# Two residual blocks on one core: the scatter matmuls of an expert group move into the next group's first product

## The chip, the core and the metric

The kernel runs on one core of a Trainium2 chip. The metric is the time of one execution on the device, in microseconds; the number compared is the median of several runs. The engines are TensorE (PE, with its weight loads as PEld), VectorE (DVE), ScalarE (ACT), GpSimd (POOL) and SyncE (SP, whose queue issues nearly all loads from HBM). The engines run side by side and wait for each other through semaphores; each takes its own instructions in the order in which they were written out for it.

## The reference, cut to what matters

The reference has two blocks of two layers each, on 256 tokens of width 1024. The change touches only the mixture of experts that ends each layer of the second block. Its first layer applies it to two streams, the latent one (`x`) and the context (`xc`); its second and last layer to the latent stream alone.

```python
def expert_choice_ffn(h, w_router, w_g, w_u, w_d):
    cap = CAPACITY_FACTOR * n // N_EXPERTS            # 32 tokens for each of 16 experts
    aff = jax.nn.softmax(jnp.einsum('bnd,de->ben', h, w_router), axis=1)
    gate, idx = lax.top_k(aff, cap)
    xs = h[bi, idx]
    a = jnp.einsum('becd,edf->becf', xs, w_g)
    u = jnp.einsum('becd,edf->becf', xs, w_u)
    y = jnp.einsum('becf,efd->becd', jax.nn.silu(a) * u, w_d)
    return jnp.zeros_like(h).at[bi, idx].add(y * gate[..., None])
...
x = x + gt2 * expert_choice_ffn(h2, ...)
```

All of it is float32. Each expert has three weight matrices of 1024 x 1024, so a layer's experts are 192 MB (16 x 3 x 4 MB) that are read once.

## The kernel before, in words

**Groups, products, steps.** The 16 experts go in four groups of four (`GE`), `gi` from 0 to 3. A group has three products: gate (`w_e_gate`), up (`w_e_up`) and down (`w_e_down`). A product runs over the contraction in four steps (`kp`, L1280); in a step there is one weight tile of 1024 KB for each of the four experts. On each tile stand, for each stream `s`, four matmuls (two rows of blocks `k`, two halves `n` of the output's 1024 columns), so with two streams a step has 32 matmuls and with one 16.

**Quarters.** An expert has 32 tokens, so a matmul (L1290) has 32 columns of weights: it fills a quarter of the array, and expert `e` of the group always has quarter `e`, its result in rows 32e to 32e+31 of an accumulator. A stream has two accumulators of 512 columns; with two streams three come from the pool `acc` (three buffers) and one from `mm`.

**Between the products.** ScalarE takes the silu of the gate product (L1303, recorded at L278 in the helper `act`), VectorE multiplies it by the up product (L1312), TensorE transposes the result (L1316) and ScalarE copies it (L1317); that is the left side of the down product.

**The scatter.** ScalarE copies the down product into `ys` (L1332), a buffer of the pool `k4`, for each stream. `scatter` (L1321) then adds it into the stream: for each of eight blocks `k` of 128 features one matmul of `ys` with the map of this group (L1324; the map holds each token's gate at its slot, 128 x 256), full array width, into one of three buffers `dd`, and one VectorE instruction that multiplies by the modulation and adds to `x` or `xc` (L1325). With two streams there are 16 of them behind a group's down product, with one 8. The last group (L1336) goes another way: its down product is made in four column pieces, with the scatter of two blocks per stream behind each.

**The loads.** `expert_loads` makes the list of 192 tiles in the order in which they are used, and the ring of buffers that they go to (`w`, `k8`, `hh`, `hl`, and pairs of half tiles in `k4`). `self.more` (L1284) issues them on SP (L1249). SP's queue is in order: a load that waits for its buffer holds all that are behind it.

**What sets the order.** The code is not run in the order written: a scheduler of the framework orders the instructions of each engine by its own estimate of when each may start, with the code's order as the tie. So where a matmul stands on TensorE is read from the built order and not from the code.

The names below: `w`, `k`, `hh`, `hl` on the right of an arrow of L1290 are weight tiles, `wl` the transposed left side of the down product, `k` or `pt` behind the comma the gathered tokens of the context and of the latent stream.

Of the kernel before, what the change touches and what calls it, by code (L numbers as in the profile page):

```python
# [13 lines left out]
OP = mybir.AluOpType  # L14
# [3 lines left out]
P = 128  # L18
S = 256
D = 1024  # L20
KT = D // P
# [113 lines left out]
class Kernel:  # L135
# [1138 lines left out]
    def experts(self, l, groups, gather, done):  # L1274
        nc, io = self.nc, self.io
        ns = len(groups)

        def product(which, gi, lhs):
            accs = [[self.acc(), self.acc()], [self.acc(), self.mm()]] if ns == 2 else [[self.acc(), self.acc()]]
            for kp in range(4):  # L1280
                if gather and which == 0 and gi == 0:
                    for _ in range(3 if kp == 0 else 2):
                        next(gather)
                self.more(max(0, GE - len(self.loaded)))  # L1284
                tiles = [self.loaded.pop(0) for _ in range(GE)]
                for s in range(ns):
                    for k in range(2):
                        for n in range(2):
                            for e in range(GE):
                                nc.tensor.matmul(accs[s][n][32 * e:32 * e + 32], lhs(s, 2 * kp + k, e),  # L1290
                                                 tiles[e][k][:, 512 * n:512 * n + 512],
                                                 start=kp == 0 and k == 0, stop=kp == 3 and k == 1,
                                                 skip_group_check=True)
            return accs

        for gi in range(N_EXP // GE):
            pick = lambda s, k, e: groups[s][2][k // 4][:, k % 4, (GE * gi + e) * CAP:(GE * gi + e + 1) * CAP]
            acts, actt = [], []
            pa = product(0, gi, pick)
            for s in range(ns):  # L1300
                a = self.wh([P, D], F32)
                for n in range(2):
                    self.act(a[:, 512 * n:512 * n + 512], pa[s][n], AF.Silu)  # L1303
                acts.append(a)
            pu = product(1, gi, pick)
            if gi == 0:
                maps = [self.gate_map(g[3]) for g in groups]
            for s in range(ns):
                tt = self.wl([P, KT, P], F32)
                for n in range(2):  # L1310
                    a = acts[s][:, 512 * n:512 * n + 512]
                    nc.vector.tensor_tensor(a, a, pu[s][n], op=OP.mult)  # L1312
                    ps = self.dd((P, 4, P))
                    for i in range(4):
                        b = slice(i * P, (i + 1) * P) if gi == N_EXP // GE - 1 else self.paired(i)
                        nc.tensor.transpose(ps[:, i], a[:, b], self.c("ident"))  # L1316
                    nc.scalar.copy(tt[:, 4 * n:4 * n + 4], ps)  # L1317
                actt.append(tt)
            down = lambda s, k, e: actt[s][:, k, 32 * e:32 * e + 32]

            def scatter(s, k, y):  # L1321
                x, gate, _, _ = groups[s]
                ps = self.dd()
                nc.tensor.matmul(ps, y[:, k * P:(k + 1) * P], maps[s][:, gi], start=True, stop=True)  # L1324
                nc.vector.scalar_tensor_tensor(x[:, k], ps, gate[:, k:k + 1], x[:, k], op0=OP.mult, op1=OP.add)  # L1325

            ys = [self.k4([P, D]) for _ in range(ns)]
            if gi < N_EXP // GE - 1:
                py = product(2, gi, down)
                for s in range(ns):  # L1330
                    for n in range(2):
                        nc.scalar.copy(ys[s][:, 512 * n:512 * n + 512], py[s][n])  # L1332
                    for k in range(KT):
                        scatter(s, k, ys[s])
                continue
            for q in range(4):  # L1336
                self.more(max(0, GE - len(self.loaded)))
                tiles = [self.loaded.pop(0) for _ in range(GE)]
                for s in range(ns):
                    ps = self.acc((P, S))  # L1340
                    for k in range(KT):
                        for e in range(GE):
                            nc.tensor.matmul(ps[32 * e:32 * e + 32], down(s, k, e), tiles[e][k], start=k == 0,
                                             stop=k == KT - 1, skip_group_check=True)
                    nc.scalar.copy(ys[s][:, 256 * q:256 * q + 256], ps)
                    for k in range(2 * q, 2 * q + 2):
                        scatter(s, k, ys[s])
                    for k in range(2 * q, 2 * q + 2):
                        done(s, k)

# [179 lines left out]
```

## Time and profile before

| | us |
|---|---|
| median of 3 runs | 2745.01 (2744.41 to 2746.25) |
| the profiled execution | 2746.57 |
| its span, first to last instruction | 2744.8 |
| TensorE matmul busy | 2556.2 (93%) |
| TensorE weight loads busy | 1813.3 (66%) |
| VectorE busy | 1361.8 (50%) |
| ScalarE busy | 1079.1 (39%) |

The experts of layer 0 run from about 1455 to 1960 us of the span, those of layer 1 from about 2320 to the end. A busy share is an average: matmuls overlap in the pipeline and, where they fill only a quarter of the array, run beside each other, so "busy" says that at least one quarter has work. An idle time is put down to what ended it; "issue" is idle time that ends without anything that the profile shows.

### The profile page before, as it was taken

How to read it: one execution, taken by the hardware profiler on the slowest of the kernel's cores; microseconds unless marked ns; L12 is line 12 of the kernel's file. 1: busy time of each engine (PE TensorE's matmuls, PEld its weight loads, DVE VectorE, ACT ScalarE, POOL GpSimd, SP SyncE). 2: the span in 40 equal slices, each digit the busy share in tenths (PEclk: the TensorE clock that was granted, in tenths of full speed). 3: DMA queues.
4: the chain of work that ended last, by engine and by line, in shares of the span. 5: the costliest groups of instructions: out<-in, count | busy, mean ns of one | idle time of the engine just before them, and what ended most of it. 6: DMA issues, size and time to landing. Idle time of an engine off the chain costs nothing.

```text
span 2744.8 us, 45167 instructions
## 1 busy us (share of the span) xinstructions
PE 2556.2 (93%) x18730; PEld 1813.3 (66%) x18730; DVE 1361.8 (50%) x2607; ACT 1079.1 (39%) x2073; POOL 74.9 (3%) x84
## 2 busy tenths in 40 slices
PE   7998999999999999989999999999989998888877
PEld 5998998888998789868983333333578993222222
DVE  5989977757777855787551011010487552000001
ACT  4665555555556744566452000000476442000000
POOL 0000000001000000100021000000000001000000
PEclk8999999999999999999999999999999999999998
DMA  8887954677555578423656999999732776999999
GB/s 320 273 308 272 332 174 155 206 285 256 174 186 181 194 247 282 146 78 116 184 187 239 357 409 398 425 380 410 270 108 96 220 247 261 425 424 425 424 425 323
DMA packets 315004, 742.66 MB, mean 271 GB/s; under 512 B 16215, under 2 KB 212783, under 8 KB 275119
## 3 DMA queue, kind: packets, MB, share of 16 engines
q1 hardware_dynamic: 313710, 738.72, 72.8%
q8 instruction: 148, 2.42, 0.3%
q10 hardware_dynamic: 1088, 1.05, 0.1%
q14 instruction: 58, 0.47, 0.0%
HBM read 738.67 MB, written 1.05 MB: 269 GB/s over the span
## 4 chain that ended last, share of the span: by engine, by line
PE 72%; DMA 16%; DVE 5%; ACT 4%; issue 1%; SPq 1%; POOL 0%; ACTq 0%; DVEq 0%; POOLq 0%
PE dd L254 36%; PE acc L1290 11%; PE mm L1290 5%; PE acc L254 3%; DMA k<-in_w_e_down_dram 3%; DMA w<-in_w_e_up_dram 3%; DMA k<-in_w_e_up_dram 2%; DMA k<-in_w_e_gate_dram 2%; DMA w<-in_w_e_down_dram 2%; DMA w<-in_w_e_gate_dram 2%; PE mm L1001 2%; PE ad L415 2%; ACT k L278 1%; ACT wh L236 1%; PE mm L995 1%; PE acc L973 1%
## 5 line engine op out<-in xcount | busy, mean ns | idle before, releaser
L237 DVE TENSOR_TENSOR wl<-w,wh 128x1024 fp32r<-128x1024 f32 (+1 forms) x534 | 553.1, 1038 | 282.4 <-ACT wh L236 272.9
L254 PE MATMUL dd<-hh,wh 128*128 128x256 f32 x2384 | 679.2, 287 | 14.8 <-ACT hh L278 11.7
L236 ACT CAST wh<-w 128x1024 fp32r<-128x1024 f32 (+1 forms) x534 | 479.0, 901 | 516.6 <-PE dd L254 379.4
L254 PE MATMUL dd<-hl,wh 128*128 128x256 f32 x2384 | 674.2, 283 | 1.7 <-DVE hl L500 1.7
L254 PE MATMUL dd<-hh,wl 128*128 128x256 f32 x2384 | 674.3, 283 | 0.6 <-DVE wl L237 0.6
L254 PEld LDWEIGHTS dd<-hh,wh 128*128 128x128 f32 x2384 | 451.3, 190 | 35.8 <-ACT hh L278 13.2
L254 PEld LDWEIGHTS dd<-hl,wh 128*128 128x128 f32 x2384 | 452.9, 190 | 6.5 <-DVE hl L500 2.7
L254 PEld LDWEIGHTS dd<-hh,wl 128*128 128x128 f32 x2384 | 452.5, 190 | 4.7 <-issue 2.8
L1290 PE MATMUL acc<-w,pt 128*32 128x512 f32 x624 | 223.4, 601 | 30.3 <-DMA w<-in_w_e_up_dram 16.4
L1312 DVE TENSOR_TENSOR wh<-wh,acc 128x512 f32<-128x512 f32 x20 | 13.7, 687 | 451.4 <-PE acc L1290 451.4
L1290 PE MATMUL acc<-k,pt 128*32 128x512 f32 x692 | 224.9, 598 | 8.6 <-DMA k<-in_w_e_up_dram 5.2
L254 PE MATMUL dd<-k,wh 128*128 128x256 f32 x896 | 163.5, 283 | 0.0
L1290 PE MATMUL acc<-w,k 128*32 128x512 f32 x480 | 159.9, 600 | 0.7 <-ACT pt L1187 0.7
L1290 PE MATMUL acc<-w,wl 128*32 128x512 f32 x396 | 139.7, 599 | 13.9 <-DMA w<-in_w_e_down_dram 13.9
L1290 PE MATMUL acc<-k,wl 128*32 128x512 f32 x432 | 146.4, 599 | 4.6 <-DMA k<-in_w_e_down_dram 4.6
L254 PEld LDWEIGHTS dd<-k,wh 128*128 128x128 f32 x896 | 137.5, 188 | 3.3 <-ACT pt L278 1.3
L1290 PE MATMUL acc<-k,k 128*32 128x512 f32 x376 | 134.1, 606 | 0.0
L1290 PEld LDWEIGHTS acc<-w,pt 128*32 128x32 f32 x624 | 46.0, 110 | 133.0 <-issue 69.9
L254 PE MATMUL dd<-k,wl 128*128 128x256 f32 x448 | 125.5, 280 | 0.0
L1325 DVE SCALAR_TENSOR_TENSOR x_res<-dd,mod,x_res 128x256 f32<-128x256 f32 x64 | 28.9, 483 | 171.4 <-PE dd L1324 171.3
L1290 PEld LDWEIGHTS acc<-k,pt 128*32 128x32 f32 x692 | 45.9, 109 | 95.4 <-issue 64.3
L1317 ACT COPY wl<-dd 128x512 f32<-128x512 f32 x24 | 13.2, 591 | 242.7 <-PE dd L1316 242.7
(361 smaller groups left out, 4441.1 us busy)
## 6 DMA issues: line engine op xcount, KB each, us to landing
w<-in_w_in_dram SPq DMA_DIRECT2D x104, 1024.0 KB
w<-in_w_ada_dram SPq DMA_DIRECT2D x63, 1024.0 KB
w<-in_w_e_gate_dram SPq DMA_DIRECT2D x54, 1024.0 KB
w<-in_w_e_up_dram SPq DMA_DIRECT2D x54, 1024.0 KB
w<-in_w_e_down_dram SPq DMA_DIRECT2D x48, 1024.0 KB
w<-in_w_up_dram SPq DMA_DIRECT2D x44, 1024.0 KB
k<-in_w_e_gate_dram SPq DMA_DIRECT2D x43, 1024.0 KB
k<-in_w_e_down_dram SPq DMA_DIRECT2D x43, 1024.0 KB
```

Of the source, the lines that this page charges most:

```text
L236: self.nc.scalar.copy(h, src)
L237: self.nc.vector.tensor_tensor(l, src, h.bitcast(F32), op=OP.subtract)
L254: self.last_mm = self.nc.tensor.matmul(ps, a, b, start=first and i == 0, stop=last and i == len(ops) - 1, skip_group_check=group)
L278: i = self.nc.scalar.activation(out, in_, func, **kw)
L415: nc.tensor.matmul(ad[32 * g:32 * g + 32], cs[:, 2 * c + j], t[:, j, 256 * g:256 * g + 256], start=j == 0 and (c == 0 or not hold), stop=j ...
L973: nc.tensor.matmul(ps[:, :n], q[:, f, mt, qb * P:(qb + 1) * P], kk[br][i][:, f, lo:512], start=i == 0, stop=i == 1 and not mask, skip_grou ...
L995: nc.tensor.transpose(pp[:, i], e[:, i * P:(i + 1) * P], self.c("ident"))
L1001: nc.tensor.matmul(po[64 * f:64 * f + 64], vv[:, kt, P * br + 64 * f:P * br + 64 * f + 64], pt[:, f, i], start=i == 0, stop=i == len(kts) ...
L1290: nc.tensor.matmul(accs[s][n][32 * e:32 * e + 32], lhs(s, 2 * kp + k, e), tiles[e][k][:, 512 * n:512 * n + 512], start=kp == 0 and k == 0, ...
L1312: nc.vector.tensor_tensor(a, a, pu[s][n], op=OP.mult)
L1317: nc.scalar.copy(tt[:, 4 * n:4 * n + 4], ps)
L1325: nc.vector.scalar_tensor_tensor(x[:, k], ps, gate[:, k:k + 1], x[:, k], op0=OP.mult, op1=OP.add)
```

## The change

The scatter of a group that is not the last is no longer written behind its down product. The 16 (or 8) of them are put in a list, block by block and with the streams in turn, and `product` takes a quarter of the list after each of its steps: four per step with two streams, two with one. The next product is the next group's gate product, so all are written within its four steps. `scatter` moves out of the loop and takes the group's number; the last group's scatters are called as before.

```diff
                                                  skip_group_check=True)
+                for _ in range(min(len(rest), KT * ns // 4)):
+                    scatter(*rest.pop(0))
             return accs
+
+        rest = []
+
+        def scatter(gi, s, k, y):
+            x, gate, _, _ = groups[s]
+            ps = self.dd()
+            nc.tensor.matmul(ps, y[:, k * P:(k + 1) * P], maps[s][:, gi], start=True, stop=True)
+            nc.vector.scalar_tensor_tensor(x[:, k], ps, gate[:, k:k + 1], x[:, k], op0=OP.mult, op1=OP.add)
...
                     for n in range(2):
                         nc.scalar.copy(ys[s][:, 512 * n:512 * n + 512], py[s][n])
-                    for k in range(KT):
-                        scatter(s, k, ys[s])
+                rest += [(gi, s, k, ys[s]) for k in range(KT) for s in range(ns)]
                 continue
...
-                        scatter(s, k, ys[s])
+                        scatter(gi, s, k, ys[s])
```

What the scheduler makes of it on TensorE, in layer 0, between the down product of group 0 and the gate product of group 1. Before, the last three of the 16 scatters and what follows them; the four tiles of the step are `w_17872`, `w_17874`, `k_3122_17876` and `k_3123_17878`:

```order
L1324 MATMUL dd_17859<-k_3062_17597,k_3078_17649 128x256
L1324 MATMUL dd_17862<-k_3062_17597,k_3078_17649 128x256
L1324 MATMUL dd_17865<-k_3062_17597,k_3078_17649 128x256
L1290 MATMUL acc_17868<-w_17872,k_2926_16882 32x512
L1290 MATMUL acc_17868<-w_17874,k_2926_16882 32x512
L1290 MATMUL acc_17868<-k_3122_17876,k_2926_16882 32x512
L1290 MATMUL acc_17868<-k_3123_17878,k_2926_16882 32x512
L1290 MATMUL acc_17869<-w_17872,k_2926_16882 32x512
L1290 MATMUL acc_17869<-w_17874,k_2926_16882 32x512
L1290 MATMUL acc_17869<-k_3122_17876,k_2926_16882 32x512
L1290 MATMUL acc_17869<-k_3123_17878,k_2926_16882 32x512
```

After, at the same place (a scatter is L1303 here); the same four tiles are now `w_17824`, `w_17826`, `k_3106_17828` and `k_3107_17830`, and five more L1290 on the first two stand ahead of these rows, directly behind the down product:

```order
L1290 MATMUL acc_17822<-w_17826,pt_17209 32x512
L1290 MATMUL mm_17823<-w_17824,pt_17209 32x512
L1290 MATMUL mm_17823<-w_17826,pt_17209 32x512
L1303 MATMUL dd_17866<-k_3053_17576,k_3077_17648 128x256
L1303 MATMUL dd_17869<-k_3062_17597,k_3078_17649 128x256
L1303 MATMUL dd_17872<-k_3053_17576,k_3077_17648 128x256
L1303 MATMUL dd_17875<-k_3062_17597,k_3078_17649 128x256
L1303 MATMUL dd_17918<-k_3053_17576,k_3077_17648 128x256
L1290 MATMUL acc_17820<-k_3106_17828,k_2926_16882 32x512
L1290 MATMUL acc_17821<-k_3106_17828,k_2926_16882 32x512
L1290 MATMUL acc_17822<-k_3106_17828,pt_17209 32x512
L1290 MATMUL mm_17823<-k_3106_17828,pt_17209 32x512
```

The scatters now stand among the step's own matmuls, and the four tiles, which took turns before, come in pieces: the first two tiles, five scatters, the third tile alone. In full, the first two steps read: 8 matmuls on the first two tiles, 5 scatters, 4 on the third tile, 4 scatters, the step's other 20 (eight of them on the fourth tile), 2 scatters, 4 and 4 on the second step's first two tiles, 5 scatters, the rest.

The same place one group later, between group 1 and group 2. Before, the last two scatters and the first of the gate product, whose tiles are `hh`, `w`, `k_3212` and `hl`:

```order
L1324 MATMUL dd_18452<-k_3062_17597,k_3168_18239 128x256
L1324 MATMUL dd_18455<-k_3062_17597,k_3168_18239 128x256
L1290 MATMUL acc_18458<-hh_18462,k_2926_16882 32x512
L1290 MATMUL acc_18458<-w_18464,k_2926_16882 32x512
L1290 MATMUL acc_18458<-k_3212_18466,k_2926_16882 32x512
L1290 MATMUL acc_18459<-hh_18462,k_2926_16882 32x512
L1290 MATMUL acc_18459<-w_18464,k_2926_16882 32x512
```

After, from the last of the first block of five scatters to the second block, which has seven:

```order
L1303 MATMUL dd_18508<-k_3053_17576,k_3167_18238 128x256
L1290 MATMUL acc_18410<-k_3196_18418,k_2926_16882 32x512
L1290 MATMUL acc_18411<-k_3196_18418,k_2926_16882 32x512
L1290 MATMUL acc_18412<-k_3196_18418,pt_17209 32x512
L1290 MATMUL mm_18413<-k_3196_18418,pt_17209 32x512
L1303 MATMUL dd_18511<-k_3062_17597,k_3168_18239 128x256
L1303 MATMUL dd_18514<-k_3053_17576,k_3167_18238 128x256
```

Here too one tile's matmuls stand alone between two blocks of scatters. In group 2 the blocks have 5, 7 and 4, in group 3 they have 7, 5 and 4. From the third step of each gate product on, the rows of before and after agree up to the buffers' numbers. In layer 1 the eight scatters of a group stand behind the first two tiles' matmuls instead of ahead of them, seven of them in one block.

## Rows read from the trace of the kernel before

**Rows 1.** Busy time by stretch, two products each, layer 0; last: clock, DMA share, GB/s.
```profile
1713.00:1789.40 76.40, 76.40 (x514) 24.32 (x513) 2.60 (x5) 2.39 (x4) 0.00 (x0) 1.00 1.01 425
1838.00:1912.70 74.70, 74.70 (x514) 23.67 (x514) 2.59 (x5) 3.67 (x5) 0.00 (x0) 1.00 1.01 406
```

**Rows 2.** DMA issues of the whole program, one line: count and size of one.
```profile
w<-in_w_e_gate_dram SPq DMA_DIRECT2D x54, 1024.0 KB
```

**Rows 3.** Who waited for whom, 1560 to 1920 us: total, times, longest.
```profile
PEld acc L1290 <- issue: 128.4, 431, 0.3
PEld mm L1290 <- issue: 87.7, 304, 0.3
PEld dd L1324 <- ACT k L1332: 2.5, 3, 0.8
```

**Rows 4.** Waits of SP's queue, 1440 to 1990 us: total, times, longest.
```profile
SPq L1249 <- PE mm L1290: 288.9, 36, 27.8
```

**Rows 5.** Timeline of TensorE, last step of a down product: start, duration.
```profile
1571.85 0.59 PE L1290 MATMUL acc<-hh,wl 128*32 128x512 f32 x1
1572.28 0.59 PE L1290 MATMUL acc<-hh,wl 128*32 128x512 f32 x1
...
1572.71 0.59 PE L1290 MATMUL acc<-hh,wl 128*32 128x512 f32 x1
1572.71 0.62 PE L1290 MATMUL acc<-w,wl 128*32 128x512 f32 x1
...
1573.57 0.59 PE L1290 MATMUL acc<-hh,wl 128*32 128x512 f32 x1
...
1574.46 0.62 PE L1290 MATMUL acc<-k,wl 128*32 128x512 f32 x1
```

**Rows 6.** Timeline of TensorE, first scatter and the starts of the four steps.
```profile
1582.24 1.02 PE L1290 MATMUL mm<-hl,wl 128*32 128x512 f32 x2
1583.19 2.00 PE L1324 MATMUL dd<-k,k 128*128 128x256 f32 x8
...
1590.54 0.62 PE L1290 MATMUL acc<-w,k 128*32 128x512 f32 x2
...
1597.43 0.60 PE L1290 MATMUL acc<-w,k 128*32 128x512 f32 x2
...
1606.11 0.59 PE L1290 MATMUL acc<-k,k 128*32 128x512 f32 x1
...
1615.67 0.59 PE L1290 MATMUL acc<-hl,k 128*32 128x512 f32 x1
```

**Rows 7.** Chain of work that ended last, layer 0, scatters and transposes: start, us.
```profile
1583.26 7.35 PE dd L1324 x32
...
1665.30 2.12 PE dd L1316 x16
...
1705.78 7.24 PE dd L1324 x32
...
1789.45 2.15 PE dd L1316 x16
...
1830.77 7.24 PE dd L1324 x32
...
1912.68 1.97 PE dd L1316 x16
```

**Rows 8.** The page's group of additions, and the timeline of ScalarE's copies.
```profile
L1325 DVE SCALAR_TENSOR_TENSOR x_res<-dd,mod,x_res 128x256 f32<-128x256 f32 x64 | 28.9, 483 | 171.4 <-PE dd L1324 171.3
...
1579.87 0.58 ACT L1332 COPY k<-acc 128x512 f32<-128x512 f32 x1 [0.27 <-PE acc L1290]
1582.44 0.58 ACT L1332 COPY k<-acc 128x512 f32<-128x512 f32 x1 [1.99 <-PE acc L1290]
```

**Rows 9.** Busy time in a stretch of layer 1, columns as in rows 1.
```profile
2480.00:2520.00 40.00, 33.05 (x146) 9.83 (x144) 3.55 (x8) 1.17 (x2) 0.00 (x0) 1.00 1.01 425
```

**Rows 10.** Who waited for whom, 2330 to 2745 us.
```profile
PEld acc L1290 <- DMA w<-in_w_e_up_dram: 33.1, 19, 2.7
```

More of the change, by code (lines that the diff above doesn't have):

```diff
@@ L1319, in experts @@
             down = lambda s, k, e: actt[s][:, k, 32 * e:32 * e + 32]
[L1321 to L1325, printed above, removed]
             ys = [self.k4([P, D]) for _ in range(ns)]
```

## The prediction

> **What bounds the kernel now.** Six views, in this order. First the busy time by stretch, for the experts of layer 0, where two streams (context and latent) share each weight tile. From the end of one group's scatter to the next group's transposes TensorE is busy all the time and the loads run at 425 and 406 GB/s [rows 1]. At 425 GB/s a tile of 1024 KB [rows 2] takes 2.47 us, a step of four 9.9 us, so engine and loads are close to each other, and the reader must see which of them ends last. The second view, who waited for whom between 1560 and 1920 us, tells it: TensorE waited for no load there. Its wait is "issue", 128.4 and 87.7 us in pieces of at most 0.3 us [rows 3]. The third, the waits of the load queue, shows the other side: 288.9 us in which SP waited for one of L1290's accumulations to give a buffer back [rows 4]. TensorE is the bound in layer 0, and the loads follow it.
>
> What "issue" is stands in the fourth view, the timeline of TensorE [rows 5]. A matmul of L1290 fills a quarter of the array (32 columns, one expert each) and has two records 0.43 us apart, so 0.86 us. The order there is three matmuls on the first expert's tile (hh), three on the second's (w), the fourth of each, then the third's (k) and the fourth's (hl). The first two of hh start at 1571.85 and 1572.71; w starts at 1572.71, when the second of hh starts, and before the third of hh (1573.57), which stands ahead of it. The third expert's tile begins at 1574.46. One rule covers all of this: within a quarter one matmul follows the other at 0.86 us; the engine goes on to other quarters while one matmul waits for its quarter, but not past a second. A step in which the order goes round the quarters 0 1 2 3 then takes 8 x 0.86 = 6.9 us; a step whose order takes one tile after the other takes 8.6 to 9.6. The first three steps after the scatter start at 1590.54, 1597.43 and 1606.11, the fourth at 1615.67: 6.89, 8.68 and 9.56 us [rows 6].
>
> The fifth view, the chain, gives the pieces that are moved: 32 records of scatter at 1583.26, 1705.78 and 1830.77, about 7.25 us each, and the transposes of the following group at 1665.30, 1789.45 and 1912.68 [rows 7]. Counting the order of before by the rule, with 0.46 us for a scatter matmul (7.35/16 in the first), I get 122.1 and 121.3 us between transposes; measured are 124.15 and 123.23. The count is 2 us short in each, of which the short waits for ACT in [rows 3] are a part. It is good to 2%, and its shortfall is the same in every group, so a difference of two counts should be better than that.
>
> The sixth view is layer 1. There one stream uses each tile, the loads stand at 425 GB/s, and TensorE waits for each tile, up to 2.7 us [rows 9, 10].
>
> **The change part by part.** It removes no instruction and adds none: 48 scatter matmuls of layer 0 (3 groups of 16) and 24 of layer 1 move, each with its addition on VectorE.
>
> Layer 0, the matmuls. A scatter matmul is 128 columns wide. Before, it starts at 1583.19, when the last quarter's two records (from 1582.24, 0.86) are over, and the first L1290 after it comes at 1590.54, when the block is done [rows 6]. So each block empties all quarters. Before there is one block per group, behind the last product, and the product after it starts with four tiles present and an order that goes round the quarters. In the change's order the 16 stand in four blocks (5, 4, 2, 5) within the first two steps of group 1; in blocks of 5, 7, 4 in group 2; 7, 5, 4 in group 3. Between the blocks stand the matmuls of one tile alone, or of two, and the other quarters have nothing.
>
> I count from the end of the last product to the start of the third step, behind which the orders agree up to the next scatter; a place is one matmul of a quarter, 0.857 us. Group 1 before: the block 7.36, the first step's 8 places 6.86, the second step 8.61, together 22.8 us (in the trace 1583.19 to 1606.11, 22.9). After: two tiles abreast, started before the last product ends, 2.6; block of 5, 2.3; one tile alone, 4 x 0.857 = 3.4; block of 4, 1.8; the fourth tile's eight in a row, 6.9; block of 2, 0.9; second step's first two tiles, 6 places, 5.1; block of 5, 2.3; eight places to the third step, 6.9. Sum 32.3, so +9.4. Group 2 before: 22.8. After: 2.6 + 2.3 + 3.4 + 3.2 (block of 7) + 11 places, 9.4 + 1.8 + 8 places, 6.9 = 29.7, so +6.9. Group 3 before: 21.1 (its second step goes round three quarters). After: 3.5 + 3.2 + 9.4 + 2.3 + 3.4 + 1.8 + 6 places, 5.1 = 28.8, so +7.7.
>
> Together +24.0 us. With seven more blocks come seven more changes between quarters and full width. The one before cost 0.09 us (1583.10 to 1583.19) going in and at most 0.1 coming back (1590.54 against 1583.19 + 16 x 0.452, the pace of the second and third block) [rows 6, 7]. I take 0.1 for each, 0.7 us; the bounds are 0 and 2.
>
> That the count lets a matmul pass a waiting one rests on w at 1572.71 ahead of hh at 1573.57 [rows 5].
> The Trainium skill (TensorE: Matmul & The Clock Gate, Part 3, The mechanism) states the opposite for matmuls in tiles of the array: they start and end strictly in program order. By the rows the change costs 24.0 us here, by that rule 29.1; the trace speaks against the rule, and it is the last of the rivals.
>
> What hides, and what if not. The additions on VectorE are 483 ns each [rows 8] against 0.46 us for a matmul, behind three buffers; the largest block is 7 now, 16 before, so they gain room: 0. The copies of the product on ACT freed the first scatter in before, 2.5 us over three waits [rows 3], but the quarters were not empty then either (1583.10): 0. The next product's first matmuls need accumulators that these copies free; the second was copied at 1579.87, well before the last product ended, the third from 1582.44 [rows 8], so at most one copy, 0.6 us a group, and I take 0. SP: the product's buffers are held two steps longer, and the two half tiles loaded into the same pool go to other places or come later than the last scatter: 0, with one tile, 2.5 us, as the other end. A loss of 24 us gives the loads slack that they lacked, so no load should be late.
>
> Layer 1. The eight scatters of a group stand in one block but for one, behind the first two tiles' matmuls instead of ahead of them. TensorE waits for every tile there, so a few us earlier or later go into these waits: 0. The last group has no scatter moved behind its own product, so the tail is as it was.
>
> Sum. 24.0 + 0.7 = +24.7 us. On the profiled execution (2746.57 us for a span of 2744.8) that is 2771.3; this execution stands 1.6 us above the median of the runs, so the median comes to 2769.7 us. Nothing after layer 0 can take the loss back: the loads of the next mixer wait in SP's one queue behind the experts' own, and the mixer needs the sums.
>
> **The rivals.**
> The scatters vanish in TensorE's idle quarters: faster. For it: 216 us of "issue" in layer 0 alone [rows 3]. If all three blocks, 21.8 us, went there, the loads would become the bound: 48 tiles x 2.47 = 118.6 us against 123.7, so at most 5.1 a group, 15 in all: 2730 us. Against it: a full-width matmul needs all quarters empty [rows 6]. It decides if quarter matmuls run beside a scatter.
> The loss is taken back: no change, 2745 us. The end is set by loads at 425 GB/s in layer 1 [rows 9]; if these began at the same moment as before, 24 us would vanish there. Against it: their buffers are freed by the mixer of layer 1, which starts only with the sums of layer 0.
> Loads come late as well. The first step holds its tiles for 20 us instead of 7, so buffers come back 10 us later in each group. If PE then catches up with loads that need 9.9 us a step against its 9.5, up to 10 us a group are added, halved for what the slow steps gain: 2785 us. Against it: SP waited for PE and not PE for a load [rows 3, 4].
> Strict order. If no matmul passed a waiting one, each wait for a quarter would hold all: counted so, the change costs 29.1 us, 2774.8 with the switches. That count gives 156 us between transposes for before, where 124 are measured [rows 7].
>
> **How the numbers follow.** Forecast 0.86 (own range 2765 to 2773: 1.5 us for the count's fit, 0 to 2 for the switches, 2 for what the next stage may absorb); vanish 0.03; taken back 0.05; late loads 0.03; strict order 0.03. A measurement tells 0.2%, 5.5 us, from no change. Faster 0.03, same 0.05, slower 0.92. The range 2762 to 2774 leaves out the four rivals, 0.14, and a little of the forecast's own ends; it reaches 3 us below the forecast's own range towards the case that is taken back, and 1 towards the two beyond.
>
> **What would show it.** Right: transposes of layer 0 lie 131 to 133 us apart instead of 124; scatter records stand in 4, 3 and 3 blocks, with stretches between them in which one tile's matmuls follow each other at 0.86 us; PE still waits for no load in layer 0, and the loads' rate there falls by some 6%; layer 1 has its 425 GB/s, all of it 25 us later. Wrong: L1290 records starting within a block of scatters; waits of TensorE for gate tiles at a group's start; or the 25 us gone by the first full-rate load of layer 1.

## The result, and the profile after

| | before | after |
|---|---|---|
| median, us | 2744.73 (4 runs, 2744.41 to 2746.25) | 2774.62 (4 runs, 2769.84 to 2776.69) |
| profiled execution, us | 2746.57 | 2776.69 |
| its span, us | 2744.8 | 2774.9 |

The ratio is 1.0105, 95% interval 1.0093 to 1.0118: slower by 29.9 us, about 1.1%. The forecast was +24.7, at 2769.7 us; its direction and its place are right, the size is 5 us short, and the measured median stands 0.6 us above the upper end of the range that was given, 2762 to 2774.

The chain of work that ended last, kernel after, layer 0 (start, duration, engine, tile, line, records; a scatter is L1303 now and has two records, a transpose is L1326):

```profile
1587.13 2.41 PE dd L1303 x10
1593.09 1.98 PE dd L1303 x8
1602.05 1.06 PE dd L1303 x4
1608.41 2.41 PE dd L1303 x10
1676.88 2.11 PE dd L1326 x16
1721.10 2.36 PE dd L1303 x10
1727.01 3.26 PE dd L1303 x14
1739.89 1.92 PE dd L1303 x8
1809.60 2.12 PE dd L1326 x16
...
1941.08 1.97 PE dd L1326 x16
```

Against the single blocks of 32 records of before [rows 7] there are blocks of 5, 4, 2, 5 scatters and of 5, 7, 4. The blocks together take little more than the one did: 7.86 us in group 1 against 7.35. Most of the lost time is between them. The transposes of groups 1 to 2 and 2 to 3 are 132.72 and 131.48 us apart; before, 124.15 and 123.23.

The timeline of TensorE, kernel after, start of group 1's gate product (start, duration, engine, line, operation, records):

```profile
1587.06 2.48 PE L1303 MATMUL dd<-k,k 128*128 128x256 f32 x10
1589.47 1.90 PE L1290 MATMUL acc<-k,k 128*32 128x512 f32 x4
1591.21 1.02 PE L1290 MATMUL acc<-k,pt 128*32 128x512 f32 x2
1592.07 1.02 PE L1290 MATMUL mm<-k,pt 128*32 128x512 f32 x2
1593.02 2.04 PE L1303 MATMUL dd<-k,k 128*128 128x256 f32 x8
...
1601.98 1.13 PE L1303 MATMUL dd<-k,k 128*128 128x256 f32 x4
1608.34 2.48 PE L1303 MATMUL dd<-k,k 128*128 128x256 f32 x10
1610.74 1.90 PE L1290 MATMUL acc<-k,k 128*32 128x512 f32 x4
...
1617.70 0.59 PE L1290 MATMUL acc<-k,k 128*32 128x512 f32 x1
```

Where before the first step after the scatter had four quarters at once [rows 6], here the third tile stands alone from 1589.47 to 1593.02: four matmuls, eight records 0.43 us apart, 3.55 us with three quarters of the array empty. No L1290 starts within a block. The third step begins at 1617.70. TensorE counts as busy through all of it, which is why its share says nothing here.

Who waited for whom, 1560 to 1945 us, kernel after (total, times, longest), answering to [rows 3]:

```profile
PEld acc L1290 <- issue: 139.5, 463, 0.3
PEld mm L1290 <- issue: 93.7, 322, 0.3
...
PEld acc L1290 <- ACT k L1336: 2.1, 3, 0.7
...
PEld acc L1290 <- DMA k<-in_w_e_down_dram: 0.2, 1, 0.2
```

TensorE waits for a load once, 0.2 us, in group 1's down product. The row above it is new: three times a matmul of the next gate product waits 0.7 us for ScalarE's copy of the down product. SP waits longer for the accumulations that give its buffers back than in [rows 4]; its queue, 1440 to 2020 us:

```profile
SPq L1249 <- PE mm L1290: 318.1, 38, 27.9
```

Busy time by stretch, kernel after: the late steps of groups 2 and 3 (as rows 1), a whole group from transposes to transposes, and layer 1 (as rows 9):

```profile
1742.00:1809.50 67.50, 67.50 (x432) 21.14 (x430) 2.36 (x4) 2.39 (x4) 0.00 (x0) 1.00 0.93 378
1875.00:1941.00 66.00, 66.00 (x425) 20.62 (x424) 2.62 (x5) 3.67 (x5) 0.00 (x0) 1.00 0.98 377
1676.90:1809.60 132.70, 132.70 (x817) 45.49 (x817) 9.85 (x20) 6.83 (x12) 0.00 (x0) 1.00 0.95 386
2509.00:2549.00 40.00, 33.56 (x146) 9.55 (x144) 3.60 (x8) 1.17 (x2) 0.00 (x0) 1.00 1.01 425
```

The same whole group in the kernel before:

```profile
1665.30:1789.40 124.10, 124.10 (x817) 44.29 (x817) 9.84 (x20) 6.82 (x12) 0.00 (x0) 1.00 0.99 412
```

The same 817 records of matmuls in 132.7 us instead of 124.1; the loads fall from 412 to 386 GB/s because they follow TensorE. Layer 1 has its 425 GB/s [rows 9].

Where the time went, by matched instructions: after lies 0.4 us behind before at group 0's transposes, 11.6 at group 1's, 20.1 at group 2's, 28.4 at group 3's, 29.2 at layer 1's last transposes and 30.1 at the end of the span. So 28.0 us were lost in three groups of layer 0, in parts of 11.15, 8.57 and 8.25.

### The profile page after: what moved, and what is told of

Its sections match the earlier page's. It is cut to its first block, busy times and chain, and to the rows that moved or that the text cites. A ratio compares the mean times of both kernels' runs of the same rounds, so it can differ in the third digit from the quotient of the medians.

```text
span 2774.9 us, 45160 instructions
## 1 busy us (share of the span) xinstructions
PE 2590.5 (93%) x18730; PEld 1820.1 (66%) x18730; DVE 1362.2 (49%) x2607; ACT 1079.8 (39%) x2073; POOL 74.9 (3%) x84
## 4 chain that ended last, share of the span: by engine, by line
PE 73%; DMA 15%; DVE 5%; ACT 4%; issue 1%; SPq 1%; POOL 0%; ACTq 0%; DVEq 0%; POOLq 0%
PE dd L254 36%; PE acc L1290 12%; PE mm L1290 5%; PE acc L254 3%; DMA k<-in_w_e_up_dram 3%; DMA k<-in_w_e_down_dram 2%; DMA w<-in_w_e_up_dram 2%; DMA w<-in_w_e_down_dram 2%; DMA k<-in_w_e_gate_dram 2%; DMA w<-in_w_e_gate_dram 2%; PE mm L1001 2%; PE ad L415 2%; ACT k L278 1%; PE mm L995 1%; PE acc L1346 1%; PE acc L973 1%
## 5 line engine op out<-in xcount | busy, mean ns | idle before, releaser
L254 PE MATMUL dd<-hh,wh 128*128 128x256 f32 x2384 | 677.8, 286 | 14.8 <-ACT hh L278 11.7
L1290 PE MATMUL acc<-w,pt 128*32 128x512 f32 x624 | 227.5, 601 | 28.1 <-DMA w<-in_w_e_up_dram 15.9
L1290 PE MATMUL acc<-k,pt 128*32 128x512 f32 x692 | 227.7, 597 | 8.8 <-DMA k<-in_w_e_up_dram 5.3
L1290 PE MATMUL acc<-w,k 128*32 128x512 f32 x480 | 166.2, 600 | 0.7 <-ACT pt L1187 0.7
L1290 PE MATMUL acc<-k,wl 128*32 128x512 f32 x432 | 148.6, 609 | 6.0 <-DMA k<-in_w_e_down_dram 6.0
L1290 PE MATMUL acc<-w,wl 128*32 128x512 f32 x396 | 140.8, 604 | 12.7 <-DMA w<-in_w_e_down_dram 12.7
L1290 PE MATMUL acc<-k,k 128*32 128x512 f32 x376 | 137.0, 603 | 0.0
L1290 PEld LDWEIGHTS acc<-w,pt 128*32 128x32 f32 x624 | 46.2, 110 | 127.4 <-issue 67.3
L278 ACT ACTIVATE wh<-acc 128x512 f32<-128x512 f32 x20 | 11.9, 597 | 270.1 <-PE acc L1290 270.1
L1290 PEld LDWEIGHTS acc<-k,pt 128*32 128x32 f32 x692 | 46.5, 109 | 105.3 <-issue 71.9
```

Source lines behind the costliest of these rows:

```text
L254: self.last_mm = self.nc.tensor.matmul(ps, a, b, start=first and i == 0, stop=last and i == len(ops) - 1, skip_group_check=group)
L278: i = self.nc.scalar.activation(out, in_, func, **kw)
```

## The experiments

The theory: what costs is the order of the matmuls. Scatters between quarter matmuls leave quarters empty; deferring the scatters, the buffers held longer and layer 1 cost nothing. The rivals: the deferral itself makes loads late, or layer 1 carries a part, or the engine is strictly in order. In the first two kernels the quarter matmuls of layer 0 are tied to the order of the code (a tie for the scheduler, without a wait on the chip). Line numbers move with each edit: below, L1297 is the product's matmul, L1314 the scatter's, L1315 the addition on VectorE (DVE) and L1339 the transposes'. The runs of before beside these eight had medians of 2748.36 (13 runs) and 2748.22 us (16 runs), spread over 2740.75 to 2752.24, so ratios are given, and the traces decide what is under 5 us.

**turns_before: the kernel before, with the order round the quarters.**

```diff
+        prev = []
+
+        def link(i):
+            if ns == 2:
+                if prev:
+                    self.order(prev[-1], i)
+                prev[:] = [i]
...
+                                i = nc.tensor.matmul(accs[s][n][32 * e:32 * e + 32], lhs(s, 2 * kp + k, e),
...
+                                link(i)
```

> The kernel before, with one thing added: in layer 0 the quarter matmuls of every product are held in the order of the code, which goes round the quarters 0 1 2 3 within a row of blocks and a half; the scatters stay in one block behind the down product. Passing rule (a matmul waits only for its own quarter, the engine passes one waiting matmul): a step takes 8 places, 6.9 us, so TensorE needs about 92 us a group, the loads (48 tiles at 2.47 us, 118.6 us a group) become the bound, and the kernel is 12 to 16 us faster than before, about 2730 us; transposes of layer 0 lie 118 to 119 us apart instead of 124, and TensorE now waits for loads there. If something other than the order makes the steps of 8.7 to 9.6 us (the reading of tiles, the weights of 32 columns), the time stays at 2745 and the transposes at 124.

2732.37 us, ratio 0.9947 (0.9929 to 0.9965). Transposes of layer 0 are 120.9, 118.8 and 120.7 us apart. Waits, 1560 to 1940 us, and busy time by stretch:

```profile
PEld acc L1297 <- DMA w<-in_w_e_up_dram: 25.8, 15, 2.4
PEld acc L1297 <- DMA k<-in_w_e_up_dram: 14.1, 6, 2.4
PEld acc L1297 <- DMA w<-in_w_e_down_dram: 11.0, 5, 3.5
```
```profile
1660.00:1776.00 116.00, 100.82 (x800) 31.39 (x794) 9.09 (x19) 4.87 (x9) 0.00 (x0) 0.99 1.01 424
```

TensorE, busy for the whole of a group before, is now idle for 15 of 116 us and waits for tiles; the loads stand at 424 GB/s. The distances are the 118.6 us that 48 tiles need at 425 GB/s, with up to 2.3 us on top. The order alone moved the bound from TensorE to the loads.

**turns_after: the changed kernel with the same tie on its quarter matmuls, and on its scatters.**

```diff
-            nc.tensor.matmul(ps, y[:, k * P:(k + 1) * P], maps[s][:, gi], start=True, stop=True)
+            i = nc.tensor.matmul(ps, y[:, k * P:(k + 1) * P], maps[s][:, gi], start=True, stop=True)
+            if gi < N_EXP // GE - 1:
+                link(i)
```

> The changed kernel, with its layer-0 product matmuls and its deferred scatters held in the order of the code: round the quarters 0 1 2 3, four scatters behind each of the four steps of the next gate product. Theory (the loss of the change is that the order, with scatters between, leaves quarters empty, and not the deferral or its buffers): TensorE needs about 92 us a group, loads bound it, 2728 to 2733 us, the same as the kernel before with this order within 0.2%. Rival (the deferral itself costs: buffers held two steps longer make loads late): 10 us or more above the kernel before with this order, with waits of TensorE for gate tiles at a group's start.

2729.61 us, ratio 0.9933 (0.9917 to 0.9949), with four blocks of four scatters per group. It differs from turns_before by 2.8 us, 0.1%, less than can be told. One group, transposes to transposes:

```profile
1655.00:1774.40 119.40, 105.28 (x817) 33.75 (x816) 9.75 (x20) 6.82 (x12) 0.00 (x0) 0.99 1.01 424
```

Deferring the scatters over four steps costs nothing here. TensorE's share of that is hidden, since it idles 14 us of this group in any case; what the run shows is that the buffers held longer do not make the loads slower. This kernel and the changed one differ by the order alone, and their ratios, 0.9933 and 1.0105, lie 1.7% or some 47 us apart. It has the lowest median of the versions run here and is faster than both kernels.

**l0_only and l1_only: the deferral in one layer alone.**

```diff
-                rest += [(gi, s, k, ys[s]) for k in range(KT) for s in range(ns)]
+                todo = [(gi, s, k, ys[s]) for k in range(KT) for s in range(ns)]
+                if ns == 2:
+                    rest += todo
+                else:
+                    for s in range(ns):
+                        for k in range(KT):
+                            scatter(gi, s, k, ys[s])
```

This is l0_only; in l1_only the condition is `ns == 1`.

> Only the scatters of layer 0 are deferred; those of layer 1 stand behind their down product as before. Theory (the whole loss is the order in layer 0): 28 to 29 us slower than before, about 2773, transposes of layer 0 131 to 133 us apart. Rival (part of the loss beyond the counted 24 is layer 1's): 2 to 5 us less than the changed kernel.

> Only the scatters of layer 1 are deferred; layer 0 has the order of before. Theory (TensorE waits for tiles in layer 1, so a few us earlier or later go into these waits): 0 to +1 us against before, 2745 to 2746. Rival (layer 1 carries the part of the loss that the count lacks): +2 to +5 us.

l0_only: 2778.35 us, ratio 1.011 (1.0092 to 1.0129), which is 30.0 us; l1_only: 2747.09 us, ratio 1.0 (0.9989 to 1.0012). The chain of l0_only at the transposes of groups 1 to 3, 132.48 and 131.48 us apart:

```profile
1680.26 2.12 PE dd L1326 x16
...
1812.74 2.11 PE dd L1326 x16
...
1944.22 1.97 PE dd L1326 x16
```

The loss is layer 0's: l1_only cannot be told from before. From layer 1's first transposes to its last, before takes 356.6 us, the changed kernel 356.7, l1_only 356.6: the term of 0 for layer 1 is right to 0.1 us.

**pairs: two matmuls of a quarter in a row.**

```diff
-                        for n in range(2):
-                            for e in range(GE):
+                        for n, e in ((n, e) for e in range(GE) for n in range(2)):
```

The rest is as in turns_after.

> The changed kernel with its layer-0 product matmuls and scatters held in a written order, as in the run with turns, but the order within a row of blocks is 0 0 1 1 2 2 3 3: two matmuls of the same quarter follow each other, so every second one stands in front of a waiting one. Passing rule (the engine goes past one waiting matmul, not past a second): 90.3 us of TensorE a group, the loads bound, about 2730 us, the same as with turns. Strict rule (no matmul starts before the one ahead of it): 178 us a group instead of 119, so three to four groups times 59, 2900 us or more.

2733.26 us, ratio 0.994 (0.992 to 0.996). The timeline of TensorE, a down product's first matmuls; the written order is two on `k`, two on `w`, two on the next `k`, two on `hh`:

```profile
1662.83 0.62 PE L1297 MATMUL acc<-k,wl 128*32 128x512 f32 x1
1662.83 0.62 PE L1297 MATMUL acc<-w,wl 128*32 128x512 f32 x1
1662.85 0.62 PE L1297 MATMUL acc<-k,wl 128*32 128x512 f32 x1
1662.86 0.62 PE L1297 MATMUL acc<-hh,wl 128*32 128x512 f32 x1
...
1663.71 0.59 PE L1297 MATMUL acc<-k,wl 128*32 128x512 f32 x1
1663.71 0.59 PE L1297 MATMUL acc<-w,wl 128*32 128x512 f32 x1
```

All four quarters begin within 0.03 us, though the second matmul on each tile, which starts only at 1663.71, stands ahead of the next tile's first. Strict order falls: by it this kernel had to be above 2900 us. The rule gets sharper: one matmul may wait in each quarter, three waiting at once here, and the engine still goes on.

**alternate: sixteen blocks of one scatter.**

```diff
+                turn = ns == 2 and len(rest) > 0
...
+                                if turn:
+                                    link(i)
+                            if turn:
+                                link(scatter(*rest.pop(0)))
```

> Layer 0 only: of the sixteen scatters of a group one stands behind each round of quarters 0 1 2 3 in the first two steps of the next gate product: sixteen blocks of one instead of one of sixteen (before) or three to four (the change). Nothing waits for a copy at the group's start. By the count alone 117.0 us a group against 122.1 and 121.3 before, together 14.8 us less up to the transposes of group 3. If a block costs 0.1 us of switching, as predicted, 45 more blocks add 4.5: 10 us faster than before, 2735. If it costs 0.24, as the changed kernel's block edges read, 10.8: 4 us faster, 2741. If the block's edge empties the quarters at 0.5 or more, 22: 8 us slower, 2753.

2754.23 us, ratio 1.0017 (1.0007 to 1.0027), about 5 us slower; from group 0's transposes to group 3's +6.2 us against before. The timeline of TensorE, where one scatter follows each round of four quarters:

```profile
1588.07 0.70 PE L1314 MATMUL dd<-k,k 128*128 128x256 f32 x2
1588.70 0.62 PE L1297 MATMUL acc<-w,k 128*32 128x512 f32 x2
...
1589.15 0.60 PE L1297 MATMUL acc<-w,k 128*32 128x512 f32 x2
...
1589.69 0.70 PE L1314 MATMUL dd<-k,k 128*128 128x256 f32 x2
```

From scatter to scatter 1.62 us, where a place and a scatter make 0.857 + 0.452 = 1.31: a change to full width and back costs 0.31 us, three times what was predicted and a little above the 0.23 read from the longer blocks of the changed kernel. 45 more blocks make 14.0 us, against the 14.8 that the count saves. New waits, 1560 to 1940 us:

```profile
PEld dd L1314 <- DVE k L1315: 15.1, 18, 0.8
...
PEld acc L1297 <- DMA k<-in_w_e_gate_dram: 3.7, 2, 2.3
PEld acc L1297 <- DMA hl<-in_w_e_gate_dram: 2.3, 1, 2.3
```

The waits for VectorE's additions (a second row has as much again) are no cost: scatter to scatter it is 1.62 us where the scatter waits so and where it does not. The waits for loads are: from the start of the down product's last record to the first scatter it takes 1.38 us in group 1, but 4.48 and 3.61 in the other two, together 5.3 us more. -14.8 + 14.0 + 5.3 = 4.5 of the 6.2 us; 1.7 stay unexplained. This fits the third outcome by its time, but not its reason: the block's edge is 0.31 and not 0.5, and the late loads, a rival of which the changed kernel shows 0.2 us, make up most of the difference. Why these tiles are late was not tried.

**block_turns: deferred, in one block.**

```diff
+                turn = ns == 2 and which == 0 and gi > 0 and kp < 2
+                if turn:
+                    while rest:
+                        link(scatter(*rest.pop(0)))
...
+                                if turn:
+                                    link(i)
```

> The changed kernel, but the sixteen scatters of a layer-0 group stand in one block at the head of the next gate product, and the matmuls of its first two steps go round the quarters behind it; from the third step on the scheduler's order as in all the others. By the count 118.7 and 120.4 us a group against 122.1 and 121.3 before and 129.0 in the changed kernel; 7.0 us less than before up to the transposes of group 3, so 2738 us. If the deferral or its longer held buffers cost anything by themselves (the rival), 2745 or above.

2741.4 us, ratio 0.9972 (0.996 to 0.9983), 6.8 us faster against 7.0 counted. The chain at the transposes of groups 1 and 2:

```profile
1662.38 2.11 PE dd L1339 x16
...
1782.79 2.15 PE dd L1339 x16
```

They are 120.4 us apart, 3.7 less than before, with 3.4 counted; those of groups 2 and 3 are 122.2 apart, 1.1 less, with 0.9 counted. The method of counting is confirmed on an order that it had not been fitted to. On the deferral itself the run says little: the block stands where it stood before, directly behind the down product, and only the order behind it is new.

**copy_twice: the copy that a matmul waits for, made twice.**

```diff
                         nc.scalar.copy(ys[s][:, 512 * n:512 * n + 512], py[s][n])
+                        if s == 1 and n == 0:
+                            nc.scalar.copy(ys[s][:, 512 * n:512 * n + 512], py[s][n])
```

> The changed kernel, but in layer 0 the copy of the down product's third accumulator (latent stream, first half) is made twice, one after the other, on ACT: 0.59 us more until this accumulator is free for the next gate product. If the wait for this copy at a group's start is paid by TensorE (0.7 us a group, the term predicted at 0), the wait doubles to about 1.3 us a group and layer 0 grows by 3 x 0.6 = 1.8 us against the changed kernel, 2776. If the engine works past it, 0: 2774.6, with the transposes of groups 1 to 3 at the same distances as in the changed kernel.

2777.11 us, ratio 1.0106 (1.0088 to 1.0124): by the time alone no difference from the changed kernel can be told. The trace can. The wait, 1560 to 1940 us, and the timeline of ScalarE:

```profile
PEld acc L1290 <- ACT k L1338: 4.0, 3, 1.4
```
```profile
1588.84 0.58 ACT L1336 COPY k<-acc 128x512 f32<-128x512 f32 x1 [1.99 <-PE acc L1290]
1589.46 0.58 ACT L1338 COPY k<-acc 128x512 f32<-128x512 f32 x1
```

The wait goes from 2.1 to 4.0 us. From the start of a down product's last record to the first scatter, the changed kernel takes 3.96, 4.01 and 4.02 us, this one 4.58, 4.63 and 4.60: together the 1.8 us that were counted. The copy stands on the path. (The two profiled executions differ by 9.4 us in their spans; the rest lies elsewhere, most of it before group 0's down product ends and between the layers, and is not the copy's.)

## Why the prediction was right, and what was mis-sized

**The bound and the rule: right.** TensorE bound layer 0 by its order. Turning the quarters round moved the bound to the loads, with the same work and the same scatters (turns_before). The rule for passing a waiting matmul, read from [rows 5], holds per quarter (pairs) and counted block_turns to a fraction of a microsecond.

**The +24.0 of the count: right.** Its three parts, 9.4, 6.9 and 7.7, stand against 11.15, 8.57 and 8.25 measured; nearly all of what is missing lies in two terms that were taken too small.

**The copies, predicted 0: wrong.** "At most one copy, 0.6 us a group, and I take 0" had nearly the right bound and chose the wrong end. The third accumulator's copy by ScalarE, kernel after:

```profile
1580.29 0.59 ACT L1336 COPY k<-acc 128x512 f32<-128x512 f32 x1 [0.27 <-PE acc L1290]
1582.87 0.59 ACT L1336 COPY k<-acc 128x512 f32<-128x512 f32 x1 [1.99 <-PE acc L1290]
```

The second row is that copy. It ends at 1583.46, and the gate product's first matmul into that accumulator starts at 1583.56. I argued that the second copy comes long before the end; but the change puts the latent stream's matmuls of the first tile directly behind the down product, and they need the third. Before, the 7 us of scatters lay between. The weight loads at this place:

```profile
1583.50 0.11 PEld L1290 LDWEIGHTS acc<-w,pt 128*32 128x32 f32 x1 [0.70 <-ACT k L1336]
1583.51 0.14 PEld L1290 LDWEIGHTS acc<-w,k 128*32 128x32 f32 x2
```

The second tile's first matmul (`k`), in another quarter, starts only with the waiting one: a wait for another engine is not passed as a wait for a quarter is. The waits add up to 2.1 us in three groups, and copy_twice shows that they are on the path. What they add to the count is less. From the end of the last product to the first scatter the count had 2.6, 2.6 and 3.5 us, and 3.44, 3.49 and 3.50 are measured: 0.9 us in each of groups 1 and 2, nothing in group 3, where the count already had the longer time. So the term is 1.7 us.

**The switches, predicted 0.1: mis-sized.** Changed kernel: 0.09 us in (1607.39 and two records at 0.43, 1608.25, to 1608.34) and 0.14 out (1608.34 to 1610.74, less five scatters at 0.452), 0.23 a block; alternate has 0.31. Seven more blocks are 1.6 to 2.2 us instead of 0.7, about the upper bound that was given. Before, only the change into the block was visible by itself; the way out was read from one place, as "at most 0.1", where the prediction's own numbers give 0.12 (1590.54 against 1590.42).

24.0 + 1.7 + 1.6 to 2.2, and the one wait of 0.2 for a load, is 27.5 to 28.1; measured in layer 0, 28.0.

**Layer 1, predicted 0: right** to 0.1 us. **The rest.** Of the 30.1 us between the two profiled executions, 2.1 lie outside layer 0's three groups: 0.4 before group 0's transposes, 0.7 in layer 1's mixer, 0.1 in its experts, 0.9 behind the last transposes. Between the last transposes of layer 0 and the first of layer 1 the ten kernels took 423.7 to 427.4 us, without a pattern, so the 0.7 there is within what single executions differ by; that the other 1.4 are the same was not shown.

**The rivals.** The scatters did not vanish: no matmul runs beside one. The loss was not taken back behind layer 0. One load was late in the changed kernel, by 0.2 us. Strict order came out near the time, 2774.8 against 2774.62, and is wrong nonetheless: by it the transposes of the changed kernel would lie some 166 us apart (156 for before, and a third of 29.1), where 132 are measured, and pairs would stand above 2900 us. A mechanism's total can fit while the mechanism doesn't hold; the distances and an order made to split the two decided it.

**The signs.** Transposes 131 to 133 us apart instead of 124: 132.7 and 131.5 (from group 0's first to group 1's, which the forecast had not read, 137.4 against 126.2). Blocks of 4, 3, 3: yes. One tile's matmuls at 0.86 us between them: yes. No wait for a load: one, of 0.2 us. Loads some 6% slower in layer 0: 412 to 386 GB/s, 6.3%. Layer 1 25 us later: 29.

## What to carry to other kernels

Where small matmuls fill only a part of the array, read the order in which TensorE gets them and ask in each stretch how many of the parts have work; its busy share is 100% with one part or with four. A full-width matmul between them empties all parts, so it is cheapest in few blocks, with an order behind each that goes round the parts; moving work "in between" gains nothing if the scheduler then lays the rest out tile by tile. And where a moved product follows another at once, look up which accumulator it takes next and when that one's copy ends.

## What the runs showed of the hardware

A quarter of the array is given work while matmuls for other quarters wait: with two matmuls in a row for each quarter, three waiting ones were passed and four quarters began within 0.03 us. A matmul that waited for a copy on ScalarE held the next quarter's matmul as well: both weight loads came within 0.01 us of each other, 0.7 us late. A change from quarter matmuls to one full-width matmul and back cost 0.31 us, with five full-width ones 0.23. With the quarters kept full, TensorE needs so much less than the loads that layer 0 runs at 424 GB/s with 12 to 13% of TensorE idle, and it makes no difference then whether sixteen scatters stand in one block or in four.
